# One product of 512 columns for the upper weights, in three stages of a two-block model

## The chip, the cores and the metric

The kernel runs on one core of one Trainium2 chip. The metric is the device time of one execution in microseconds (us), taken as the median of repeated runs; lower is better. The profile comes from one further execution.

## What is computed

The model has two blocks on 256 tokens of 1024 features (16 extra "meta" tokens are put in front of the first block, so that it works on 272). Everything is float32. Cut to what matters here:

```python
# first block, both layers: mixing, then an MLP; the MLP of layer 1 is touched by the change
a = relu(rmsnorm(h) @ w_up)              # 1024 -> 4096
h = h + (a * a) @ w_down                 # 4096 -> 1024

# second block, layer 0: short convolution
gb, gc, u = split(rmsnorm(x) @ w_in, 3)  # 1024 -> 3 x 1024
mix = (gb * causal_dwconv(gc * u, w_conv)) @ w_out

# second block, both layers: convolutional FFN
gate, up = split(causal_dwconv(rmsnorm(x) @ w_up, w_conv), 2)   # 1024 -> 2 x 2816
x = x + rmsnorm((silu(gate) * up) @ w_down)
```

## The kernel before

Every float32 matrix product is made of products in a reduced format (float32r). A number is split into an upper part and the rest: `hi` is the value copied into the format (ScalarE, L337 for weights, L362 for others) and `lo` is the value minus `hi` (VectorE, L338 and L363). A product is then hi·hi + hi·lo + lo·hi, all three added up in one PSUM bank by TensorE.

Two kinds of stages alternate. In the stages "weights stand still", a weight tile of 128 x 1024 holds eight blocks of 128 x 128; for each block `k` the helper `mm3` (L351) issues three products: upper weights by upper features (L352), upper weights by lower features (L353), lower weights by upper features (L354). The features lie with the feature number on the partitions, 256 tokens (272 in block one's first layer) in the columns, in the tiles `uh` and `ul`, so one weight tile costs 24 products of 256 columns and gives one tile of 128 outputs x 256 tokens in a PSUM bank. In the stages "features stand still" (`act_gemm`, L1123; helper `mm3a`, L357 to L359) 512 weight columns move past 128 tokens, so each product has 512 columns.

The weights come as a stream (`Stream`): 512 KB per weight tile by DMA into one of four `raw` buffers, split by ScalarE (L337) and VectorE (L338) some six tiles ahead, into eight pairs of buffers.

Stages that the change touches:

- `up1`: the MLP of layer 1, 32 weight tiles, `up_gemm(1, m, NM)` with `t0 = NM = 16`, PSUM name `pup`. The first four tiles are computed together, block by block, in the order in which `hg_split` (L426 on ScalarE for `uh`, L427 on VectorE for `ul`) finishes the features (L1098 to L1102). `relu_sq` (L923) drains each bank: relu (L925) and square (L926) on ScalarE, then the split into `ah` (L362, ScalarE) and `al` (L363, VectorE). The same helper serves layer 0 with 272 columns.
- `short_conv`: 16 of its 24 output tiles are weight-stationary (`psc`, helper `ws_tile`); the other 8 come from a features-stationary start (`first_tiles`, `pfb`).
- `conv_ffn`, twice: 18 gate tiles (`pg`) and 18 up tiles (`pu`) each; the first four of either kind come from `first_tiles`. A gate tile is drained by `conv`: a scaled copy (ScalarE L1284) and two shifted multiply-adds that read PSUM (VectorE L1285, L1286), then silu (ScalarE L1335). An up tile is drained by the same three, then GpSimd multiplies both (L1341), ScalarE splits off the upper part (`fah`, `fbh`, L362) and GpSimd the rest (L363).

All weight-stationary tiles of a stage take turns in four PSUM banks (tag `mm`). A bank is free for the tile after the next three when its last reader is done. The tile framework sets the waits and also fixes, before the run, the order of the instructions on each engine; instructions of several tiles are interleaved there, and each engine then takes its list in order and stops at an instruction whose input isn't ready.

The functions that the change touches:

Of the kernel before, what the change touches and what calls it, by code (L numbers as in the profile page):

```python
# [10 lines left out]
F32 = mybir.dt.float32  # L11
F32R = mybir.dt.float32r
I32 = mybir.dt.int32
AF = mybir.ActivationFunctionType
ALU = mybir.AluOpType
# [3 lines left out]
P = 128  # L19
D = 1024  # L20
KB = D // P
NM = 16
L = 272
# [250 lines left out]
def tile_forward(ctx: ExitStack, tc: tile.TileContext, wts, hT_in, pT_in, cols_in, rows_in, gsub_in, lam_in,  # L274
                 relb_in, consts_in, hot_in, out, dbg=None, stop=None):
    nc = tc.nc
    V, S, G, T = nc.vector, nc.scalar, nc.gpsimd, nc.tensor
# [11 lines left out]
    def ps(name="mm", tag="mm"):  # L289
        return banks["pool"].tile([P, 512], F32, tag=tag, name=name, bufs=banks["n"][tag])  # L290
# [58 lines left out]
    ws = Stream()  # L349

    def mm3(o, wh, wl, xh, xl, start, stop):  # L351
        T.matmul(o, wh, xh, start=start, stop=False)  # L352
        T.matmul(o, wh, xl, start=False, stop=False)  # L353
        T.matmul(o, wl, xh, start=False, stop=stop)  # L354

    def mm3a(o, xh, xl, wh, wl, start, stop):
        T.matmul(o, xh, wh, start=start, stop=False)  # L357
        T.matmul(o, xh, wl, start=False, stop=False)  # L358
        T.matmul(o, xl, wh, start=False, stop=stop)  # L359

    def split(hi, lo, src, eng=V):
        ins = S.activation(hi, src, AF.Copy)  # L362
        eng.tensor_tensor(lo, src, hi.bitcast(F32), ALU.subtract)  # L363
        return ins
# [4 lines left out]
    blk1 = ExitStack()  # L369
    main1 = blk1.enter_context(tc.tile_pool(name="main1", bufs=1, reuse_waits="tile"))  # L370
    h = main1.tile([P, KB, L], F32, name="h")
    uh = main1.tile([P, KB, L], F32R, name="uh")
    ul = main1.tile([P, KB, L], F32R, name="ul")
    R2 = main1.tile([P, L], F32, name="R2")
    mixs = ExitStack()
    ps1 = ExitStack()
# [491 lines left out]
    for pair in range(2):  # L868
        outs = [ps("pout", "mm" if m < 2 else "sm") for m in range(4)]
        for half in (1, 0):  # L870
            for j in range(2):
                wh, wl = ws.get("out", 2 * pair + j, half)
                for m in range(2):
                    o = outs[2 * j + m]
# [32 lines left out]
    def gain(name, i=0):  # L907
        g = xp.tile([P, D], F32, tag="gain", name="gain", bufs=2)
        nc.sync.dma_start(g, rows_in[row_of(name, i)].partition_broadcast(P))
        return g  # L910
# [11 lines left out]

    def relu_sq(o, m, t0):  # L923
        t = tmp1.tile([P, L], F32, tag="rl", name="rl", bufs=3)
        S.activation(t[:, t0:], o[:, t0:L], AF.Relu)  # L925
        S.activation(t[:, t0:], t[:, t0:], AF.Square)  # L926
        split(ah[m // 8][:, m % 8, t0:], al[m // 8][:, m % 8, t0:], t[:, t0:])

    def up_gemm(i, m, t0):
        wh, wl = ws.get(f"up{i}", m)  # L930
        o = ps("pup")
        for k in range(KB):
            mm3(o[:, t0:L], wh[:, k * P:(k + 1) * P], wl[:, k * P:(k + 1) * P], uh[:, k, t0:], ul[:, k, t0:], k == 0, k == KB - 1)
        relu_sq(o, m, t0)

    def split_p(raw, parts):
# [52 lines left out]
    for m in range(KB):  # L989
        o = ps("pdn")  # L990
        for g in range(4):
            wh, wl = ws.get("dn0", m, g)
# [3 lines left out]
        t = tmp1.tile([P, L], F32, tag="rl", name="dn", bufs=3)  # L996
# [44 lines left out]
    for g in (2, 3, 0, 1):  # L1041
        wh, wl = wp[g // 2]
        z = zs[g] = tmp2.tile([P, 2, L], F32, name=f"zp{g}")
        outs = []
        for m in range(2):
            o = ps("pz")
# [52 lines left out]
    for ks in ((0, 1), (2, 3), (6, 7, 4, 5)):  # L1099
        for (wh, wl), o in first:  # L1100
            for k in ks:
                mm3(o[:, NM:L], wh[:, k * P:(k + 1) * P], wl[:, k * P:(k + 1) * P], uh[:, k, NM:], ul[:, k, NM:], k == 0, k == 5)  # L1102
    for m in range(FF // P):
        if m < 4:
            relu_sq(first[m][1], m, NM)
# [79 lines left out]
    up_ = ctx.enter_context(tc.tile_pool(name="u2", bufs=1, reuse_waits="tile"))  # L1185
# [16 lines left out]
        return r  # L1202

    def new_u(name):
        return (up_.tile([P, KB, 256], F32R, tag="uh", name=name + "h", bufs=1),
                up_.tile([P, KB, 256], F32R, tag="ul", name=name + "l", bufs=1))

    def norm_T(u, t, g, r=None):

# [26 lines left out]
    def boundary(fin, u, g):  # L1236

        rr = []
        for t in range(2):
            with tc.high_priority(offset=HP):  # L1240
                fin(t)
                ins = norm_T(u, t, g)
            if t == 0:
                ws.cap = len(plan)
                with tc.issue_after(ins.ins):
                    ws.emit(ws.used + 6)
            rr.append(row_rstd(x[t]))
        return rr

    def half(a, t):  # L1250
        return a[:, :, t * P:(t + 1) * P]

    def ws_tile(key, u, o):

        wh, wl = ws.get(*key)
        for k in range(KB):
            mm3(o, wh[:, k * P:(k + 1) * P], wl[:, k * P:(k + 1) * P], u[0][:, k, :], u[1][:, k, :], k == 0, k == KB - 1)
        return o

    def first_tiles(key, ux, rr, u, g):  # L1260


        def mid():
            for t in range(2):
                norm_T(u, t, g, rr[t])

        acc = act_gemm(key, KB, lambda k, t: half(ux[0], t)[:, k], lambda k, t: half(ux[1], t)[:, k], KB, mid, bound=False)
        tok = []
        for t in range(2):
            y = big("ft")  # L1270
            for i, n in enumerate(H2):
                S.activation(y[:, n], acc[t][i], AF.Copy, scale=rr[t])
            tok.append(y)

        def block(n):
            o = ps("pfb", "acc")[:, 0:256]
            for t in range(2):
                T.transpose(o[:, t * P:(t + 1) * P], tok[t][:, n * P:(n + 1) * P], eye)
            return o
        return block  # L1280
# [7 lines left out]
    def short_conv(fin):  # L1288
        g = gain("g_pre_mix_2", 0)
        hs = ExitStack()  # L1290
        hp = hs.enter_context(tc.tile_pool(name="hidc", bufs=1, reuse_waits="tile"))
        sh = hp.tile([P, KB, 256], F32R, name="sh")
        sl = hp.tile([P, KB, 256], F32R, name="sl")
        rr = boundary(fin, (sh, sl), g)
        gp = gain("g_post_mix_2", 0)

        def tail(j, pc, pu, pb):
            gc = t2.tile([P, 256], F32, tag="f1", name="gc", bufs=3)
            S.activation(gc, pc, AF.Copy)
            V.tensor_tensor(gc, pu, gc, ALU.mult)  # L1300
            y = t2.tile([P, 256], F32, tag="f2", name="y", bufs=3)
            conv(y, gc, "sc", j)
            V.tensor_tensor(y, pb, y, ALU.mult)
            split(sh[:, j, :], sl[:, j, :], y)

        u = new_u("sc")
        block = first_tiles(("sc8",), (sh, sl), rr, u, g)
        for j in SC_ORDER:
            outs = []
            for part in (1, 2, 0):  # L1310
                if (j, part) in SC_FIRST:
                    outs.append(block(SC_FIRST.index((j, part))))
                else:
                    outs.append(ws_tile(("sci", j, part), u, ps("psc")[:, 0:256]))
            tail(j, *outs)
        acc = act_gemm(("sco",), KB, lambda k, t: half(sh, t)[:, k], lambda k, t: half(sl, t)[:, k], KB)
        hs.close()
        return post_fin(acc, gp)

    def conv_ffn(i, fin):  # L1320
        g = gain("g_pre_ffn_2", i)
        hs = ExitStack()
        hp = hs.enter_context(tc.tile_pool(name="hidf", bufs=1, reuse_waits="tile"))
        fa = [hp.tile([P, NF2 - KB, 256], F32R, name="fa" + c) for c in "hl"]
        ux = [hp.tile([P, KB, 256], F32R, name="fb" + c) for c in "hl"]

        def fpart(c, f):
            return fa[c][:, f, :] if f < NF2 - KB else ux[c][:, f - (NF2 - KB), :]
        rr = boundary(fin, ux, g)
        gp = gain("g_post_ffn_2", i)  # L1330

        def gate_tail(f, pg):
            a = t2.tile([P, 256], F32, tag="f1", name="a", bufs=3)
            conv(a, pg, f"fc{i}_", f)
            S.activation(a, a, AF.Silu)  # L1335
            return a

        def up_tail(f, pu, a):
            c = t2.tile([P, 256], F32, tag="f2", name="c", bufs=3)
            conv(c, pu, f"fc{i}_", NF2 + f)  # L1340
            G.tensor_tensor(c, c, a, ALU.mult)  # L1341
            split(fpart(0, f), fpart(1, f), c, G)

        u = new_u("ff")
        block = first_tiles(("ffu", i), ux, rr, u, g)
        for f in FFN_ORDER:
            a = gate_tail(f, block(f) if f < 4 else ws_tile(("gate", i, f), u, ps("pg")[:, 0:256]))
            up_tail(f, block(4 + f) if f < 4 else ws_tile(("upp", i, f), u, ps("pu")[:, 0:256]), a)
        acc = act_gemm(("ffd", i), NF2, lambda k, t: fpart(0, k)[:, t * P:(t + 1) * P],
                       lambda k, t: fpart(1, k)[:, t * P:(t + 1) * P], 6)  # L1350
        hs.close()
        return post_fin(acc, gp)
# [189 lines left out]
```

## Time and profile before

| | |
|---|---|
| median of 3 runs | 1258.46 us (1257.72 to 1258.51) |
| the profiled execution, its own time | 1255.57 us |
| span of its instructions | 1253.8 us |
| mean granted TensorE clock | 0.999 of full speed |
| TensorE busy | 1221.4 us of the span |
| VectorE, ScalarE, GpSimd busy | 824.1, 732.0, 216.9 us |

PE is TensorE, PEld its weight loads, DVE VectorE, ACT ScalarE, POOL GpSimd, SP the queue that issues most DMAs. A matmul's own duration overlaps that of the next one, so what a product costs in a stream is the step from one start to the next.

### The profile page before, as it was taken

Reading aid. Unit: us, or ns where it says so; the run is one execution under the profiler, and the core shown is the slowest. Engines: PE = TensorE matmul, PEld = TensorE weight load, DVE = VectorE, ACT = ScalarE, POOL = GpSimd, SP = SyncE. Lnnn points to the kernel's source line nnn. Section 1 sums busy time; section 2 is a strip of 40 time slices with the busy share of each in tenths; the row PEclk is TensorE's granted clock in tenths of the full one; section 3 lists DMA queues with packets and bytes.
Section 4 is the critical chain, followed back from the end, with each engine's and each line's share of the span. In section 5 each row is a group of like instructions: output and inputs, shape, how many; then the busy total and the mean of one; then the engine's idle time right before and its main releaser. Section 6 shows DMA issues by size and latency. Waiting matters only on the chain.

```text
span 1253.8 us, 21438 instructions
## 1 busy us (share of the span) xinstructions
PE 1221.4 (97%) x8250; PEld 1113.0 (89%) x8250; DVE 824.1 (66%) x1252; ACT 732.0 (58%) x1262; POOL 216.9 (17%) x184
## 2 busy tenths in 40 slices
PE   7999999999999999999999999999999999999997
PEld 7888899999997999887898899988789868999875
DVE  6775558555557755445775897754888867977455
ACT  7664458775345877433653676543677756765444
POOL 1454141000113000000000053410110010634001
PEclk9999999999999999999999999999999999999999
DMA  7432137555457755553753655554675337555542
GB/s 268 136 101 85 35 102 253 172 173 177 170 177 250 239 190 185 172 191 128 237 183 124 222 193 185 187 190 148 239 266 192 111 112 227 181 185 185 190 139 92
DMA packets 63461, 219.15 MB, mean 175 GB/s; under 512 B 7117, under 2 KB 9301, under 8 KB 63360
## 3 DMA queue, kind: packets, MB, share of 16 engines
q1 hardware_dynamic: 60192, 212.87, 50.5%
q10 hardware_dynamic: 2816, 4.20, 1.0%
q8 instruction: 65, 1.06, 0.3%
q0 software_dynamic: 352, 0.72, 0.2%
q14 instruction: 36, 0.29, 0.1%
HBM read 212.51 MB, written 5.26 MB: 174 GB/s over the span
## 4 chain that ended last, share of the span: by engine, by line
PE 83%; DVE 8%; issue 3%; ACT 2%; DMA 2%; POOL 2%; SPq 0%; DVEq 0%; POOLq 0%; ACTq 0%
PE acc L359 8%; PE acc L357 8%; PE acc L358 8%; PE pup L354 5%; PE pup L353 5%; PE pup L352 5%; PE pg L352 3%; PE pu L354 3%; PE pg L354 3%; PE pg L353 3%; PE pu L352 3%; PE pu L353 3%; PE pdn L352 3%; PE pdn L353 3%; PE pdn L354 3%
## 5 line engine op out<-in xcount | busy, mean ns | idle before, releaser
L338 DVE TENSOR_TENSOR lo<-raw,hi 128x1024 fp32r<-128x1024 f32 (+1 forms) x366 | 452.9, 1242 | 234.6 <-ACT hi L337 233.3
L337 ACT ACTIVATE hi<-raw 128x1024 fp32r<-128x1024 f32 (+1 forms) x380 | 398.3, 1055 | 251.5 <-PE acc L359 102.7
L352 PE MATMUL pup<-uh,hi 128*128 128x272 f32 (+1 forms) x512 | 146.1, 286 | 1.7 <-ACT uh L426 1.7
L354 PE MATMUL pup<-uh,lo 128*128 128x272 f32 (+1 forms) x512 | 146.1, 285 | 0.2 <-DVE lo L338 0.2
L353 PE MATMUL pup<-ul,hi 128*128 128x272 f32 (+1 forms) x512 | 145.8, 285 | 0.2 <-DVE ul L427 0.2
L1201 POOL TENSOR_TENSOR rs<-ss,mhalf 128x1 f32<-128x1 f32 x24 | 23.0, 960 | 485.1 <-DVE ss L1199 485.1
L352 PEld LDWEIGHTS pup<-uh,hi 128*128 128x128 f32 x512 | 96.4, 189 | 2.9 <-ACT uh L426 2.2
L354 PEld LDWEIGHTS pup<-uh,lo 128*128 128x128 f32 x512 | 96.6, 189 | 0.4 <-DVE lo L338 0.4
L353 PEld LDWEIGHTS pup<-ul,hi 128*128 128x128 f32 x512 | 96.3, 188 | 0.4 <-DVE ul L427 0.4
L1341 POOL TENSOR_TENSOR c<-c,a 128x256 f32<-128x256 f32 x44 | 59.7, 1357 | 132.7 <-DVE c L1286 132.7
L352 PE MATMUL pg<-ffh,hi 128*128 128x256 f32 x288 | 82.0, 285 | 0.0
L354 PE MATMUL pg<-ffh,lo 128*128 128x256 f32 x288 | 81.3, 282 | 0.0
L354 PE MATMUL pu<-ffh,lo 128*128 128x256 f32 x288 | 81.3, 282 | 0.0
L353 PE MATMUL pg<-ffl,hi 128*128 128x256 f32 x288 | 81.2, 282 | 0.0
L352 PE MATMUL pu<-ffh,hi 128*128 128x256 f32 x288 | 81.2, 282 | 0.0
L353 PE MATMUL pu<-ffl,hi 128*128 128x256 f32 x288 | 81.1, 282 | 0.0
L352 PE MATMUL pdn<-ah,hi 128*128 128x272 f32 x256 | 74.1, 290 | 0.0
L354 PE MATMUL pdn<-ah,lo 128*128 128x272 f32 x256 | 74.1, 289 | 0.0
L353 PE MATMUL pdn<-al,hi 128*128 128x272 f32 x256 | 73.7, 288 | 0.0
L353 PEld LDWEIGHTS pg<-ffl,hi 128*128 128x128 f32 x288 | 54.7, 190 | 0.1
L352 PEld LDWEIGHTS pg<-ffh,hi 128*128 128x128 f32 x288 | 54.7, 190 | 0.1
L354 PEld LDWEIGHTS pg<-ffh,lo 128*128 128x128 f32 x288 | 54.7, 190 | 0.0
(481 smaller groups left out, 3277.9 us busy)
## 6 DMA issues: line engine op xcount, KB each, us to landing
raw<-wts SPq DMA_DIRECT2D x378, 512.0 KB, 3.4
gain<-rows_in SPq DMA_DIRECT2D x13, 512.0 KB, 4.7
prj<-pe ACTq DMA_DIRECT2D x8, 256.0 KB, 6.2
pj<-prj SPq DMA_DIRECT2D x4, 512.0 KB, 5.0
out_dram<-x SPq DMA_DIRECT2D x8, 256.0 KB, 2.4
hank<-biasD ACTq DMA_DIRECT2D x4, 256.0 KB, 3.9
biasT<-bsb ACTq DMA_DIRECT2D x4, 256.0 KB, 3.5
biasb<-biasT SPq DMA_DIRECT2D x8, 128.0 KB, 2.7
```

The lines of the kernel that those rows point to most:

```text
L337: S.activation(hi[:, c], src[:, c], AF.Copy)
L338: (G if n in ON_POOL else V).tensor_tensor(lo[:, c], src[:, c], hi[:, c].bitcast(F32), ALU.subtract)
L352: T.matmul(o, wh, xh, start=start, stop=False)
L353: T.matmul(o, wh, xl, start=False, stop=False)
L354: T.matmul(o, wl, xh, start=False, stop=stop)
L357: T.matmul(o, xh, wh, start=start, stop=False)
L358: T.matmul(o, xh, wl, start=False, stop=False)
L359: T.matmul(o, xl, wh, start=False, stop=stop)
L1201: G.tensor_tensor(r, s[:, 3:4], mhalf[:, 0:1], ALU.pow)
L1341: G.tensor_tensor(c, c, a, ALU.mult)
```

## The change

A new helper `mm2` makes the two products with the upper weights into one of 512 columns: `uh` and `ul` become the two halves of one tile `u2`, and block `k` of both (two pieces of 256 columns) moves past the weights in one instruction, which writes both halves of the PSUM bank. The third product (lower weights by upper features) is added to the first half. A second helper, `add_halves`, then copies the second half to SBUF on ScalarE and adds the first half on VectorE. Both are used in the layer-1 `up1` stage, for the 16 `psc` tiles and for the gate tiles of both FFNs; the up tiles, the keys and queries and the layer-0 MLP keep `mm3`. In `relu_sq` the square moves from ScalarE to GpSimd where `mm2` is used. In `conv` of a gate tile the source becomes an SBUF tile.

```diff
+    def mm2(o, wh, wl, x2, start, stop):
+        T.matmul(o.rearrange("p (a t) -> p a t", a=2), wh, x2, start=start, stop=False)
+        T.matmul(o[:, 0:256], wl, x2[:, 0], start=False, stop=stop)
+
+    def add_halves(dst, o):
+        S.activation(dst, o[:, 256:512], AF.Copy)
+        V.tensor_tensor(dst, o[:, 0:256], dst, ALU.add)
...
-    uh = main1.tile([P, KB, L], F32R, name="uh")
-    ul = main1.tile([P, KB, L], F32R, name="ul")
+    u2 = main1.tile([P, 2, KB, L], F32R, name="u2")
+    uh, ul = u2[:, 0], u2[:, 1]
...
     def relu_sq(o, m, t0):
         t = tmp1.tile([P, L], F32, tag="rl", name="rl", bufs=3)
-        S.activation(t[:, t0:], o[:, t0:L], AF.Relu)
-        S.activation(t[:, t0:], t[:, t0:], AF.Square)
+        if t0:
+            add_halves(t[:, t0:], o)
+            S.activation(t[:, t0:], t[:, t0:], AF.Relu)
+            G.tensor_tensor(t[:, t0:], t[:, t0:], t[:, t0:], ALU.mult)
+        else:
+            S.activation(t, o[:, :L], AF.Relu)
+            S.activation(t, t, AF.Square)
         split(ah[m // 8][:, m % 8, t0:], al[m // 8][:, m % 8, t0:], t[:, t0:])
...
+            if t0:
+                mm2(o, *wk, u2[:, :, k, t0:], k == 0, k == KB - 1)
+            else:
+                mm3(o[:, :L], *wk, uh[:, k, :], ul[:, k, :], k == 0, k == KB - 1)
...
-                mm3(o[:, NM:L], wh[:, k * P:(k + 1) * P], wl[:, k * P:(k + 1) * P], uh[:, k, NM:], ul[:, k, NM:], k == 0, k == 5)
+                mm2(o, wh[:, k * P:(k + 1) * P], wl[:, k * P:(k + 1) * P], u2[:, :, k, NM:], k == 0, k == 5)
...
     def new_u(name):
-        return (up_.tile([P, KB, 256], F32R, tag="uh", name=name + "h", bufs=1),
-                up_.tile([P, KB, 256], F32R, tag="ul", name=name + "l", bufs=1))
+        u = up_.tile([P, 2, KB, 256], F32R, tag="u", name=name, bufs=1)
+        return u[:, 0], u[:, 1], u
...
+    def ws_pair(key, u, name, pool):
+        wh, wl = ws.get(*key)
+        o = ps(name)
+        for k in range(KB):
+            mm2(o, wh[:, k * P:(k + 1) * P], wl[:, k * P:(k + 1) * P], u[2][:, :, k, :], k == 0, k == KB - 1)
+        s = pool.tile([P, 256], F32, tag="f0", name="s" + name, bufs=4)
+        add_halves(s, o)
+        return s
...
-                    outs.append(ws_tile(("sci", j, part), u, ps("psc")[:, 0:256]))
+                    outs.append(ws_pair(("sci", j, part), u, "psc", hp))
...
-            a = gate_tail(f, block(f) if f < 4 else ws_tile(("gate", i, f), u, ps("pg")[:, 0:256]))
+            a = gate_tail(f, block(f) if f < 4 else ws_pair(("gate", i, f), u, "pg", hp))
```

## Rows read from the trace of the kernel before

**Rows 1.** The page, part 1: busy time of the engines.
```profile
PE 1221.4 (97%) x8250; PEld 1113.0 (89%) x8250; DVE 824.1 (66%) x1252; ACT 732.0 (58%) x1262; POOL 216.9 (17%) x184
```
**Rows 2.** The page, part 4: the chain that ended last, by engine.
```profile
PE 83%; DVE 8%; issue 3%; ACT 2%; DMA 2%; POOL 2%; SPq 0%; DVEq 0%; POOLq 0%; ACTq 0%
```
**Rows 3.** Windows: stretch, length, busy time (instructions) by engine, clock, DMA.
```profile
430.00:490.00 60.00, 60.00 (x510) 60.00 (x509) 33.92 (x43) 45.89 (x86) 0.00 (x0) 1.00 0.58 192
520.00:580.00 60.00, 60.00 (x262) 48.97 (x261) 25.44 (x21) 21.22 (x20) 0.00 (x0) 1.00 0.56 189
755.00:815.00 60.00, 60.00 (x506) 60.00 (x505) 43.02 (x63) 35.74 (x63) 24.79 (x22) 1.00 0.55 185
640.00:664.00 24.00, 24.00 (x204) 24.00 (x203) 16.67 (x25) 11.91 (x19) 0.00 (x0) 1.00 0.52 176
```
**Rows 4.** Groups by form, whole span: the products with the upper weights.
```profile
L353 PE MATMUL pg<-ffl,hi 128*128 128x256 f32 x288 | 81.2, 282 | 0.0
L353 PE MATMUL pup<-ul,hi 128*128 128x256 f32 x256 | 72.1, 282 | 0.2 <-DVE ul L427 0.2
L353 PE MATMUL psc<-scl,hi 128*128 128x256 f32 x128 | 36.1, 282 | 0.0
```
**Rows 5.** Timeline of TensorE, 519.8 to 521 us: start, duration, instruction.
```profile
519.79 0.39 PE L357 MATMUL acc<-hi,ah 128*128 128x512 f32 x1
...
520.92 0.39 PE L359 MATMUL acc<-hi,al 128*128 128x512 f32 x1
```
**Rows 6.** Groups by form, 424 to 495 us (`up1`): DVE and ACT.
```profile
L338 DVE TENSOR_TENSOR lo<-raw,hi 128x1024 fp32r<-128x1024 f32 x26 | 31.9, 1226 | 28.7 <-ACT hi L337 28.5
L337 ACT ACTIVATE hi<-raw 128x1024 fp32r<-128x1024 f32 x26 | 27.6, 1060 | 14.5 <-PE pup L353 14.5
L363 DVE TENSOR_TENSOR al<-rl,ah 128x256 fp32r<-128x256 f32 x26 | 11.0, 424 | 0.0
L926 ACT ACTIVATE rl<-rl 128x256 f32<-128x256 f32 x25 | 10.5, 419 | 0.8
L925 ACT ACTIVATE rl<-pup 128x256 f32<-128x256 f32 x26 | 9.5, 366 | 0.0
```
**Rows 7.** Groups, 752 to 815 us (first FFN): waits of ACT and DVE.
```profile
L1285 DVE SCALAR_TENSOR_TENSOR a<-pg,cols,a 128x255 f32<-128x255 f32 x11 | 5.3, 483 | 16.6 <-ACT a L1284 16.6
...
L362 ACT ACTIVATE fbh<-c 128x256 fp32r<-128x256 f32 x6 | 2.5, 418 | 11.9 <-POOL c L1341 11.9
```
**Rows 8.** Timelines of ACT, DVE, POOL and PE, 762 to 770 us (first FFN).
```profile
763.32 0.42 ACT L362 ACTIVATE fah<-c 128x256 fp32r<-128x256 f32 x1 [1.98 <-POOL c L1341]
...
764.20 0.48 DVE L1285 SCALAR_TENSOR_TENSOR a<-pg,cols,a 128x255 f32<-128x255 f32 x1 [1.51 <-ACT a L1284]
765.12 1.22 DVE L338 TENSOR_TENSOR lo<-raw,hi 128x1024 fp32r<-128x1024 f32 x1
765.26 0.28 PE L354 MATMUL pg<-ffh,lo 128*128 128x256 f32 x1
765.30 0.42 ACT L1335 ACTIVATE a<-a 128x256 f32<-128x256 f32 x1 [0.25 <-DVE a L1286]
766.25 0.48 DVE L1285 SCALAR_TENSOR_TENSOR c<-pu,cols,c 128x255 f32<-128x255 f32 x1
767.39 1.58 POOL L1341 TENSOR_TENSOR c<-c,a 128x256 f32<-128x256 f32 x1 [2.84 <-DVE c L1286]
769.00 0.42 ACT L362 ACTIVATE fah<-c 128x256 fp32r<-128x256 f32 x1 [1.98 <-POOL c L1341]
769.33 0.46 ACT L1284 ACTIVATE a<-pg,cols 128x256 f32<-128x256 f32 x1
```
**Rows 9.** Timeline of POOL, 732 us: a product with no split beside it.
```profile
732.81 0.73 POOL L1341 TENSOR_TENSOR c<-c,a 128x256 f32<-128x256 f32 x1 [0.92 <-DVE c L1286]
```
**Rows 10.** Timelines of ACT and DVE, 407 to 412 us (start of `up1`).
```profile
407.63 3.31 ACT L426 ACTIVATE uh<-h,cols 128x256 fp32r<-128x256 f32 x8 [0.55 <-DVE h L1087]
...
408.33 3.24 DVE L427 SCALAR_TENSOR_TENSOR ul<-h,cols,uh 128x256 fp32r<-128x256 f32 x8
```

More of the change, by code (lines that the diff above doesn't have):

```diff
@@ L932, in up_gemm @@
         for k in range(KB):
-            mm3(o[:, t0:L], wh[:, k * P:(k + 1) * P], wl[:, k * P:(k + 1) * P], uh[:, k, t0:], ul[:, k, t0:], k == 0, k == KB - 1)
+            wk = wh[:, k * P:(k + 1) * P], wl[:, k * P:(k + 1) * P]
+            if t0:
+                mm2(o, *wk, u2[:, :, k, t0:], k == 0, k == KB - 1)
+            else:
+                mm3(o[:, :L], *wk, uh[:, k, :], ul[:, k, :], k == 0, k == KB - 1)
         relu_sq(o, m, t0)
```

## Prediction

> **What bounds the kernel now.** I read the page from the top. TensorE is busy 1221.4 of 1253.8 us, the other engines far less [rows 1], and the chain that ended last runs through TensorE for 83% of the span [rows 2]; the reader should see that time can only be won where a TensorE instruction becomes cheaper, and lost where TensorE is made to wait. A busy share doesn't say what a product costs, since durations overlap, so I counted products in stretches of pure work [rows 3]. A stretch also counts the one or two products that are under way at its start, so I take two off. The layer-1 up products: 60 us / 508 = 118.1 ns from start to start. The FFN's products of 256 columns: 60 / 504 = 119.0. The short convolution's: 24 / 202 = 118.8. Products of 512 columns: 60 / 260 = 230.8. TensorE is busy through all four stretches and the granted clock is 1.00, its 2.4 GHz level; nothing is waited for there.
>
> The last views are those of the engines that drain the banks. In `up1` ScalarE works 45.9 of 60 us and VectorE 33.9; in the short convolution 11.9 and 16.7 of 24; in the FFN 35.7 and 43.0 of 60, with GpSimd 24.8 [rows 3]. So there is room in sum, but the FFN is a stage in which ScalarE and VectorE wait for each other, below.
>
> **The change on TensorE.** Each block that `mm2` takes loses one product: 256 in `up1`, 288 gate, 128 short convolution, one for each L353 instruction [rows 4], 672 in all. Two products of 256 columns become one of 512. What is saved is twice the short step minus the long one: in `up1` 236.2 − 230.8 = 5.4 ns, in the short convolution 6.8, in the FFN 7.2. That gives 256 × 5.4 + 128 × 6.8 + 288 × 7.2 = 1.4 + 0.9 + 2.1 = **4.4 us saved**. The trace of before has no product of 512 columns whose moving operand lies in two pieces, as `u2[:, :, k]` does. Bounds: nothing, if the second piece costs as much as a new product; and 672 × (5.4 to 7.2 + 4.8) = 7.6 us, if the long product runs at the fastest spacing seen, five steps in 1.13 us, 226 ns [rows 5]. I take 4.4, since the long stretch is an average over work like this.
>
> [...]
>
> **The start of `up1`.** The features come from ScalarE at one `uh` per 0.41 us from 407.63, and from VectorE at one `ul` per 0.41 us from 408.33 [rows 10]. Before, the first products needed only the first `uh`; now the first needs the first `ul` too, done at about 408.75 instead of 408.05. After that TensorE has four tiles' work per block and is behind the features. I take **0.5 us lost**; above, if the wait covers the last write into the joint tile (411.57), 3.5 us. In the other stages the features are complete long before, as features-stationary products stand between.
>
> **What the draining costs.** There are 32 + 36 + 16 = 84 new pairs of a copy and an add. The copy reads 256 columns from PSUM like L925, 0.37 us; the add is like L363's, 0.42 us [rows 6].
>
> In `up1` ScalarE's list per tile is now weights' upper part 1.06, relu 0.37, square 0.42, split about 0.42: 2.27 us [rows 6]. Copy in, square out leaves 2.22. VectorE goes from 1.23 + 0.42 to 2.07. GpSimd, idle there [rows 3], gets a square of 0.73 to 1.58 us, by GpSimd's product without and with a weight split of VectorE beside it [rows 8, 9]. A tile lasts 24 × 118.1 ns = 2.83 us, later 2.79. All fit under it. What covers them is the four banks: a bank is asked for again three tiles, 8.4 us, after its product ended, while the chain to its last reader is 0.8 us plus what it queues behind (a split of 1.06 and one of 1.23). I take nothing. In the short convolution three copies and three adds come to 24.0 / 202 × 72 = 8.5 us of TensorE work; VectorE goes from 5.9 to 7.2 us there. Nothing, again; at its end the longer tail (0.8 us) hides behind the seven earlier blocks of the next product, 7 × 6 × 0.23 = 9.7 us.
>
> **The FFN is the doubtful stage.** Follow one round [rows 8]: split 763.32, then the gate's convolution on ScalarE 0.33 later, VectorE's two steps from 764.20, a weight split at 765.12, the up tile's steps from 766.25, GpSimd at 767.39, and ScalarE's next split at 769.00, which it had waited 1.98 us for. This is a ring with no slack in it, 5.68 us long, and TensorE's round is 48 × 119.0 = 5.71 us. So the drain already runs as slowly as TensorE, 3.8 us behind it (the gate's product at 765.26 ends at 765.54; its convolution starts at 769.33). After the change TensorE's round is 5.65 us. Where the copy and the add go in the ring decides. In every round ScalarE waits 1.98 us for GpSimd and VectorE 1.5 us for the convolution [rows 7, 8], in the same stretch, and the gate's product is long done. If the copy stands ahead of that split, both fit into these waits and the ring keeps 5.68; 14 rounds at 0.03 us over TensorE's are taken up by the banks. I take this, cost nothing.
>
> **Sum.** 1255.57 − 4.4 + 0.5 = 1251.7 for the profiled execution. The median of the runs stands 2.9 us above that execution, so **1254.6 us**, 0.3% less. About 0.2%, 2.5 us, is what a measurement of this kernel tells from no change.
>
> **Rivals.**
>
> *The copy stands behind the split in ScalarE's list* (slower). Then copy, add and two hand-overs (0.1 each, as convolution to VectorE's step) lengthen the ring by 0.37 + 0.42 + 0.2 = 1.0 us at most; by less if the weight split at 765.12 moves into the new wait. From 5.65 us on the ring sets TensorE's pace. The banks give slack first: the up tile's last reader ends about 4.5 us after its product, and the bank is asked for after 8.5, so 4.0 us. With two thirds of the 1.0: (6.35 − 5.65) × 14 − 4.0 = 5.8 us per FFN, 11.6 for both: 1266. The whole 1.0 gives 1276, a half 1261. For it: today's list holds exactly such a split that waits ahead of the next gate's convolution. Against it: the copy depends on TensorE alone. Chance 0.24.
>
> *The long product costs as much as the two short ones*, its step being set by columns only or the two pieces costing a start each. Then 1258.5 + 0.5 = 1259.0, no change. For it: the short step scatters by 0.9 ns between the stages [rows 3], doubled 1.8 of the 5 to 7 ns that are to be saved. Against it: the 512-column stretch is below twice the short step in all three stages. [...] Chance 0.2.
>
> *`up1` loses its cover*: ScalarE's list in the strict order copy, relu, split of one tile, with the waits for VectorE and GpSimd in it. Then a tile costs ScalarE 1.06 + 0.37 + 0.42 + 0.42 + 0.73 + 0.42 and four hand-overs, 3.8 us, against 2.79: 32 × 1.0 − 8.4 = 24 us more, 1279. Against it: lists of several tiles are interleaved already [rows 8]. Chance 0.04.
>
> **Chances and range.** The forecast has 0.52; its own range is 1251 to 1257, of which a little lies within 0.2% of before. So faster 0.48, same 0.25, slower 0.27. The range goes from 1258.46 − 7.6 = 1250.9 up to 1268: it leaves out the top of the first rival, the third, and something better than the fastest spacing.
>
> **What would show it.** In the profile of the changed kernel: products of 512 columns into `pup`, `pg`, `psc` with steps of about 231 ns followed by one of 119; a block at 350 ns instead of 356. In the FFN the time from one `fah` split to the next, and whether the copy from `pg` stands before or after the split; TensorE idle in `pg` or `pu` products with a release by ScalarE or VectorE would be the first rival, idle in `pup` the third. The prediction is wrong if the long step is over 236 ns, if the FFN's round is above 5.7 us, or if the first products of `up1` start after 409.3.

## The result

The changed kernel takes 1298.41 us (median of 4 runs, 1297.9 to 1304.15) against 1258.09 for the kernel before, measured beside it: 40 us slower, ratio 1.0337, 95% interval 1.0309 to 1.0365 (ratios here go by all runs, not by the medians). The forecast was 1254.6, with a range up to 1268. Its sign was wrong, and the range doesn't hold the time.

The page of the changed kernel, its first part (busy time) and its fourth (the chain that ended last, by engine):

```profile
PE 1228.2 (95%) x7578; PEld 1081.8 (83%) x7578; DVE 857.3 (66%) x1336; ACT 746.4 (58%) x1314; POOL 246.3 (19%) x216
...
PE 64%; DVE 14%; ACT 8%; issue 6%; POOL 5%; DMA 2%; DVEq 0%; SPq 0%; POOLq 0%; ACTq 0%
```

The 672 products are gone (8250 to 7578 [rows 1]), yet the chain runs through TensorE for 64% of a longer span, 83% before [rows 2]; VectorE, ScalarE and GpSimd took most of the difference. The windows of the changed kernel, on stretches like those of [rows 3]:

```profile
430.00:490.00 60.00, 57.38 (x320) 48.53 (x319) 40.56 (x57) 37.20 (x76) 17.03 (x19) 1.00 0.54 171
533.00:593.00 60.00, 60.00 (x262) 48.99 (x261) 25.74 (x21) 21.75 (x21) 0.00 (x0) 1.00 0.61 193
654.00:678.00 24.00, 24.00 (x138) 20.93 (x138) 20.34 (x36) 14.57 (x27) 0.00 (x0) 1.00 0.55 177
768.00:828.00 60.00, 52.22 (x357) 47.71 (x358) 39.21 (x64) 33.80 (x62) 19.87 (x18) 1.00 0.49 157
```

In `up1` and in the FFN TensorE now has holes, 2.6 and 7.8 us in 60. No engine is full in their place: the busiest, VectorE, works 40.6 and 39.2 of 60 us, and ScalarE does *less* per 60 us than before in both stages. The short convolution is as dense as ever, and so is the features-stationary stretch. The clock is at its upper level in all four.

Where the 42 us between the two profiled spans lie, stage by stage. I took each stage from the start of its first product to the end of its last one in TensorE's timeline, and the stretches between; the first line is the length before, the others the difference to it, in us, from one profiled execution of each kernel. The lines below the second are the experiments.

| kernel | up1 | up1 to short conv. | short conv. | FFN 0 | FFN 0 to keys | FFN 1 |
|---|---|---|---|---|---|---|
| before (length) | 91.5 | 117.0 | 48.0 | 104.8 | 114.1 | 104.9 |
| **after** | +4.2 | +8.7 | −1.0 | +12.9 | +3.0 | +13.3 |
| gemm_only | −1.8 | +0.1 | −0.9 | +0.3 | +3.0 | −1.1 |
| drain_only | +4.2 | +8.1 | 0.0 | +11.8 | 0.0 | +12.4 |
| joint_tiles | +0.1 | +0.1 | 0.0 | 0.0 | +1.5 | 0.0 |
| psc_only | 0.0 | 0.0 | −1.0 | 0.0 | +3.0 | 0.0 |
| copy_first | +4.1 | +8.9 | −1.0 | +1.1 | +1.6 | +1.1 |
| late_split | +4.4 | +7.5 | −1.0 | +0.9 | +3.1 | +0.7 |
| square_act | −1.8 | 0.0 | −1.0 | +12.7 | +1.5 | +13.4 |
| vec_halves | −1.8 | −0.1 | −0.9 | +4.7 | +1.6 | +4.6 |
| square_pool | +0.2 | +10.6 | 0.0 | 0.0 | 0.0 | 0.0 |
| up1_and_sc | −0.4 | 0.0 | −1.0 | 0.0 | 0.0 | 0.0 |
| all_three | −0.2 | 0.0 | −1.0 | +1.2 | 0.0 | +1.0 |

In the changed kernel the short convolution gains 1.0, and three places lose: `up1` with its aftermath 12.9, the FFNs 26.2, the boundary to keys and values 3.0. The stretch ahead of `up1` differs by 11 us between these executions: its first product starts between 406.9 us (joint_tiles) and 417.9 us (late_split). In the two latest, drain_only and late_split, the granted clock was lower for a part of the stretch (0.55 and 0.54 in the ten microseconds from 130, 1.00 there in the kernel before). So the table starts at `up1`, and differences of one or two us are read from it rather than from the medians.

**The FFN round.** Timelines of ScalarE, VectorE, GpSimd and TensorE in the changed kernel, one round, which answers to [rows 8] (start, duration, instruction; in brackets how long the engine had been idle, and what ended that):

```profile
780.59 0.42 ACT L371 ACTIVATE fah<-c 128x256 fp32r<-128x256 f32 x1 [1.64 <-POOL c L1369]
780.91 1.04 ACT L337 ACTIVATE hi<-raw 128x1024 fp32r<-128x1024 f32 x1
781.86 0.37 ACT L362 ACTIVATE spg<-pg 128x256 f32<-128x256 f32 x1
783.58 0.51 ACT L1312 ACTIVATE a<-spg,cols 128x256 f32<-128x256 f32 x1 [1.36 <-DVE spg L363]
...
787.61 0.42 ACT L371 ACTIVATE fah<-c 128x256 fp32r<-128x256 f32 x1 [1.64 <-POOL c L1369]
...
781.99 1.23 DVE L338 TENSOR_TENSOR lo<-raw,hi 128x1024 fp32r<-128x1024 f32 x1 [2.03 <-ACT hi L337]
783.13 0.42 DVE L363 TENSOR_TENSOR spg<-pg,spg 128x256 f32<-128x256 f32 x1
...
785.77 1.22 DVE L338 TENSOR_TENSOR lo<-raw,hi 128x1024 fp32r<-128x1024 f32 x1
...
786.05 1.53 POOL L1369 TENSOR_TENSOR c<-c,a 128x256 f32<-128x256 f32 x1 [4.22 <-ACT a L1363]
...
783.60 0.51 PE L358 MATMUL pg<-ff,hi 128*128 128x512 f32 x1 [0.88 <-DVE spg L363]
```

From split to split it is 7.02 us (787.61 − 780.59), and the eight rounds behind it are 7.02 or 7.03 long; before, 5.68. Read ScalarE's list: split, weights' upper part, *then* the copy, then a wait of 1.36 us for the add, which stands on VectorE behind the lower part of those weights. Only then the convolution, silu, GpSimd's product, and the next split. The convolution began 0.33 us after the split before; it begins 2.99 us after it now. TensorE waits 0.88 us for the add (the last line), which is the bank's last reader.

**The round of `up1`.** Timelines of ScalarE, VectorE and GpSimd in the changed kernel:

```profile
459.18 0.36 ACT L362 ACTIVATE rl<-pup 128x256 f32<-128x256 f32 x1
460.89 0.42 ACT L936 ACTIVATE rl<-rl 128x256 f32<-128x256 f32 x1 [1.36 <-DVE rl L363]
...
464.29 0.42 ACT L371 ACTIVATE ah<-rl 128x256 fp32r<-128x256 f32 x1 [1.15 <-POOL rl L937]
464.62 1.04 ACT L337 ACTIVATE hi<-raw 128x1024 fp32r<-128x1024 f32 x1
465.57 0.36 ACT L362 ACTIVATE rl<-pup 128x256 f32<-128x256 f32 x1
...
459.30 1.23 DVE L338 TENSOR_TENSOR lo<-raw,hi 128x1024 fp32r<-128x1024 f32 x1 [0.53 <-ACT hi L337]
...
463.22 1.04 POOL L937 TENSOR_TENSOR rl<-rl 128x256 f32<-128x256 f32 x1 [1.21 <-ACT rl L936]
```

Two tiles take 465.57 − 459.18 = 6.39 us, 3.2 each, against TensorE's 2.8. ScalarE waits twice: 1.36 us for the add behind a weight split, 1.15 us for GpSimd's square. TensorE ran ahead on its four banks at first, so only 4.2 us show inside the stage; the other 8.7 come after it. TensorE's weight loads there, and windows of the changed kernel:

```profile
508.04 0.31 PEld L1172 LDWEIGHTS pth<-eye,h 128*128 128x128 f32 x3 [2.83 <-ACT ah L371]
511.16 0.50 PEld L1137 LDWEIGHTS pst<-ones,ssum 128*128 128x128 f32 x2 [2.81 <-DVE r2t L1138]
...
510.00:520.00 10.00, 8.84 (x34) 7.58 (x35) 4.19 (x13) 6.20 (x12) 1.23 (x2) 0.66 0.29 105
```

Two things make up the 8.7. The next stage's first steps wait 2.83 and 2.81 us for ScalarE and VectorE, which are still busy with the last tiles. Then TensorE goes on at a granted clock of 0.66, two thirds of these ten microseconds at its lower level (1.2 GHz); in the kernel before it is 1.00 there. By my estimate, half of the time that it works at the lower level, that costs between 2 and 3 us. So some 10 of the 12.9 us are the ring itself: from the first tile's split to the last tile's it takes 93.2 us instead of 83.1.

### The profile page after: what moved, and what is told of

The parts are those of the page before. It is cut to its first block, busy times and chain, and to the rows that moved or that the text cites. A ratio compares the mean times of both kernels' runs of the same rounds, so it can differ in the third digit from the quotient of the medians.

```text
span 1296.1 us, 20191 instructions
## 1 busy us (share of the span) xinstructions
PE 1228.2 (95%) x7578; PEld 1081.8 (83%) x7578; DVE 857.3 (66%) x1336; ACT 746.4 (58%) x1314; POOL 246.3 (19%) x216
## 4 chain that ended last, share of the span: by engine, by line
PE 64%; DVE 14%; ACT 8%; issue 6%; POOL 5%; DMA 2%; DVEq 0%; SPq 0%; POOLq 0%; ACTq 0%
PE acc L368 8%; PE acc L366 8%; PE acc L367 8%; DVE lo L338 5%; ACT hi L337 4%; POOL c L1369 3%; PE pdn L352 2%; PE pdn L353 2%; PE pdn L354 2%; PE pup L352 2%; PE pup L354 2%; PE pup L353 2%; PE psc L358 2%; POOL rl L937 1%; PE ptf L1236 1%
## 5 line engine op out<-in xcount | busy, mean ns | idle before, releaser
L358 PE MATMUL pg<-ff,hi 128*128 128x512 f32 x288 | 105.0, 403 | 19.3 <-DVE spg L363 19.3
L358 PE MATMUL pup<-u,hi 128*128 128x512 f32 x256 | 91.3, 398 | 5.4 <-DVE rl L363 2.4
L352 PE MATMUL pu<-ff,hi 128*128 128x256 f32 x288 | 81.3, 282 | 3.5 <-ACT a L1363 3.5
L353 PE MATMUL pu<-ff,hi 128*128 128x256 f32 x288 | 81.2, 282 | 0.0
L354 PE MATMUL pu<-ff,lo 128*128 128x256 f32 x288 | 81.2, 282 | 0.0
L359 PE MATMUL pg<-ff,lo 128*128 128x256 f32 x288 | 80.8, 281 | 0.0
L352 PE MATMUL pup<-u,hi 128*128 128x272 f32 x256 | 74.6, 291 | 0.0
L354 PE MATMUL pup<-u,lo 128*128 128x272 f32 x256 | 74.2, 290 | 0.3 <-DVE lo L338 0.3
L353 PE MATMUL pup<-u,hi 128*128 128x272 f32 x256 | 73.7, 288 | 0.0
L359 PE MATMUL pup<-u,lo 128*128 128x256 f32 x256 | 71.8, 280 | 0.0
L352 PEld LDWEIGHTS pu<-ff,hi 128*128 128x128 f32 x288 | 54.3, 189 | 6.1 <-ACT a L1363 4.7
L353 PEld LDWEIGHTS pu<-ff,hi 128*128 128x128 f32 x288 | 54.4, 189 | 0.0
L354 PEld LDWEIGHTS pu<-ff,lo 128*128 128x128 f32 x288 | 54.3, 189 | 0.0
```

The costliest lines, as they stand in the source:

```text
L358: T.matmul(o.rearrange("p (a t) -> p a t", a=2), wh, x2, start=start, stop=False)
L359: T.matmul(o[:, 0:256], wl, x2[:, 0], start=False, stop=stop)
```

## The experiments

**gemm_only.** The products of the change without its drain.

```diff
-            add_halves(t[:, t0:], o)
-            S.activation(t[:, t0:], t[:, t0:], AF.Relu)
-            G.tensor_tensor(t[:, t0:], t[:, t0:], t[:, t0:], ALU.mult)
+            S.activation(t[:, t0:], o[:, 0:256], AF.Relu)
+            S.activation(t[:, t0:], t[:, t0:], AF.Square)
...
-        s = pool.tile([P, 256], F32, tag="f0", name="s" + name, bufs=4)
-        add_halves(s, o)
-        return s
+        return o[:, 0:256]
```

> Leaves out the hi·lo part of the sum: the products are those of the change (one of 512 columns, one of 256), but each bank is drained as in the kernel before, from its first half alone, without the copy, the add and the square on GpSimd. Theory A (the new drain makes the loss, and the 512-column products do save): up1 and both FFN stages run at TensorE's pace again, FFN round 5.63 to 5.68 us, and the time is 1258.1 - 4.4 + 0.5 = 1254, plus up to 3 us that the joint tile costs at the keys-and-values boundary: 1254 to 1257. Theory B (the 512-column products or the joint feature tile make the loss): it stays above 1285.

Measured: 1257.86 us, ratio 0.9988 (0.9965 to 1.0012), 0.9 us above the range of theory A and far from B. Windows in the two FFNs:

```profile
755.00:815.00 60.00, 59.51 (x417) 55.44 (x416) 43.80 (x64) 36.26 (x64) 23.27 (x20) 1.00 0.60 185
1100.00:1150.00 50.00, 50.00 (x356) 46.90 (x354) 35.75 (x54) 29.96 (x52) 20.92 (x18) 1.00 0.60 192
```

The splits are 5.68 to 5.70 us apart in the steady part of both stages, as before (but for two of 5.9 and 6.0 us in FFN 0), although TensorE needs only 5.65 for a round now. In FFN 1 it works through the window without a hole, runs ahead of the drain on its banks and keeps the whole saving (−1.1); in FFN 0 it has holes (0.49 us in this window), its rounds are as long as the drain's, and nothing is gained. Three up tiles of FFN 0 take 3.0 to 3.4 us instead of 2.85, 1.0 us in sum; what lengthens them isn't shown. The boundary to keys loses 3.0 us in this kernel too, without any new drain.

**drain_only.** The drain of the change without its products.

```diff
+    def add_halves(dst, o):
+        S.activation(dst, o, AF.Copy)
+        V.tensor_tensor(dst, o, dst, ALU.max)
...
+            add_halves(t[:, t0:], o[:, t0:L])
+            S.activation(t[:, t0:], t[:, t0:], AF.Relu)
+            G.tensor_tensor(t[:, t0:], t[:, t0:], t[:, t0:], ALU.mult)
```

> The products and the separate feature tiles of the kernel before; only the new drain: a copy of the bank to SBUF on ScalarE, then on VectorE the larger of bank and copy (which are equal), then the rest as in the change, with the square on GpSimd. Theory A (the drain makes the loss): FFN round about 7.0 us, up1 about 3.2 us per tile, and a time of about 1258 + 13 + 13 + 13 = 1297 (1294 to 1299), without the 3 us at the keys-and-values boundary and without the saving. Theory B (products or joint tile): 1258 to 1262.

Measured: 1294.17 us, ratio 1.0289 (1.0253 to 1.0325). Theory A: +12.3 in and behind `up1`, +11.8 and +12.4 in the FFNs, a split every 7.03 us, nothing at the boundary to keys. Nearly the whole loss without one 512-column product. (The 12.3 again hold a stretch at the lower clock: 0.82 in the ten microseconds from 520.)

**joint_tiles** and **psc_only.** The joint feature tile alone, and the change in the short convolution alone.

```diff
-        return (up_.tile([P, KB, 256], F32R, tag="uh", name=name + "h", bufs=1),
-                up_.tile([P, KB, 256], F32R, tag="ul", name=name + "l", bufs=1))
+        u = up_.tile([P, 2, KB, 256], F32R, tag="u", name=name, bufs=1)
+        return u[:, 0], u[:, 1], u
```

> The kernel before with its features in one joint tile of two halves, in up1 and in the second block, and nothing else changed. Theory A: the tile is taken as one buffer, so that whatever starts early with one half now waits for both: 3 us later at the boundary to keys and values, 1261, nothing elsewhere. Rival: the 3 us come from the drains' order there, and this kernel is 1258, no change.

> The change in the short convolution alone (16 output tiles, with copy and add), with the joint tiles; up1 and the FFNs as in the kernel before. Theory A: this stage had room, its products go from 48.0 to 47.1 us, so -0.9 us there, plus what the joint tile costs at the keys-and-values boundary: 1257.2 without that cost, 1260 with it. Rival (any such drain slows its stage): above 1262.

Measured: 1260.06 us, ratio 1.0008 (0.9982 to 1.0033), and 1260.36, ratio 1.0014 (0.9994 to 1.0034): neither can be told from no change by its time. By the table the joint tile loses 1.5 us at the boundary, and 3.0 with the short convolution's change in the same program. TensorE's first product on the keys' features in joint_tiles, ScalarE ahead of it, and TensorE's next wait:

```profile
907.68 0.50 PE L357 MATMUL acc<-hi,kv 128*128 128x512 f32 x1 [1.27 <-ACT kv L362]
...
905.83 1.31 ACT L1371 ACTIVATE sgm<-acc,rs 128x512 f32<-128x512 f32 x2 [1.70 <-PE acc L359]
907.04 0.59 ACT L362 ACTIVATE kv<-ptf 128x512 fp32r<-128x512 f32 x1
...
909.78 0.73 PE L359 MATMUL acc<-hi,kv 128*128 128x512 f32 x2 [0.90 <-DVE kv L363]
```

Both sigmoids stand ahead of the first split there; before, that split stood between them. TensorE waits 1.27 us for it instead of 0.62, and 0.90 us for the lower part where it didn't wait before: together the 1.5 us. So an order on ScalarE moved because two tiles became one. Kernels that keep two tiles at this boundary (drain_only, square_pool, up1_and_sc, all_three) lose nothing. The kernels that lose 3.0 have the same two waits; what differs is the clock behind them. Windows of joint_tiles and of psc_only:

```profile
907.00:917.00 10.00, 8.42 (x39) 6.65 (x40) 9.91 (x18) 8.45 (x17) 0.64 (x2) 1.00 0.79 256
...
907.00:917.00 10.00, 8.34 (x32) 6.54 (x33) 8.65 (x16) 8.56 (x17) 0.70 (x2) 0.83 0.80 260
```

The granted clock is 0.83 behind the waits in the four kernels that lose 3.0 or 3.1 (the changed one, gemm_only, psc_only, late_split) and 1.00 in the four that lose 1.5 or 1.6 (joint_tiles, copy_first, square_act, vec_halves). Why it falls in one kernel and holds in another isn't settled.

**copy_first** and **late_split.** The change, with the FFN's split of a gated product pinned behind another instruction of ScalarE: behind the next tile's copy, or behind the next pair's first convolution steps.

```diff
+            pg = block(f) if f < 4 else ws_pair(("gate", i, f), u, "pg", hp)
+            if late:
+                with tc.issue_after(copies[-1].ins):
+                    split(*late, G)
+            a = gate_tail(f, pg)
```

> The change with one thing altered, in the FFNs: the split of a gated product is put behind the copy of the next gate tile in ScalarE's list, so that the order is weights' split, copy, split, convolution in place of split, weights' split, copy, wait for the add, convolution. Theory A (copy and add inside the ring split, copy, add, convolution, silu, GpSimd's product, split lengthen it to 7.02 us): the round falls to TensorE's 5.65 or the 5.7 of before, both FFNs win 13 us each, 1298 - 26 = 1272, and up1 stays as it is. Rival B (VectorE and GpSimd have too much work with the added operations, whatever the order): the round stays above 6.5 and the time above 1288.

> The change with one thing altered, in the FFNs: the split of a gated product is put behind the convolution's first steps of the next gate and up tile in ScalarE's list, so that no convolution waits for GpSimd any more and the ring is opened. Theory A: TensorE sets the pace, 5.63 to 5.66 us a round, 1270 to 1272, not slower than with the copy alone put first. Rival B (load of VectorE and GpSimd): round above 6.5, above 1288.

Measured: 1274.96 us, ratio 1.0134 (1.0108 to 1.0159), and 1277.13, ratio 1.0148 (1.0111 to 1.0184). Theory A in both for the stage, though the times lie 3 and 5 us above what was expected. The FFNs lose 1.1 and 1.1, or 0.9 and 0.7, in place of 13. In late_split the splits are 5.85 us apart, neither the 5.63 to 5.66 of theory A nor the 6.5 of its rival; what sets that pace isn't shown. Its four times go from 1271 to 1281 at granted clocks of 0.994 to 0.985, so the table tells more than its median. Timelines of ScalarE and GpSimd in copy_first:

```profile
817.77 0.42 ACT L373 ACTIVATE fbh<-c 128x256 fp32r<-128x256 f32 x1 [0.43 <-POOL c L1371]
819.18 0.51 ACT L1314 ACTIVATE a<-spg,cols 128x256 f32<-128x256 f32 x1 [1.00 <-DVE spg L365]
...
821.48 1.05 ACT L337 ACTIVATE hi<-raw 128x1024 fp32r<-128x1024 f32 x1
822.44 0.36 ACT L364 ACTIVATE spg<-pg 128x256 f32<-128x256 f32 x1
823.22 0.42 ACT L373 ACTIVATE fbh<-c 128x256 fp32r<-128x256 f32 x1 [0.42 <-POOL c L1371]
...
821.65 1.53 POOL L1371 TENSOR_TENSOR c<-c,a 128x256 f32<-128x256 f32 x1 [2.25 <-ACT a L1365]
```

The copy and the weights' upper part now lie in the time in which GpSimd multiplies; the round is 5.45 us, shorter than TensorE's, while the drain catches up. What is left of the loss comes while the first eight tiles are drained: two gate tiles last 3.6 and 4.1 us instead of 2.8, 2 us in sum.

**square_act** and **square_pool.** The square of `up1` moved alone: back to ScalarE in the changed kernel, over to GpSimd in the kernel before.

```diff
-            G.tensor_tensor(t[:, t0:], t[:, t0:], t[:, t0:], ALU.mult)
+            S.activation(t[:, t0:], t[:, t0:], AF.Square)
```

> The change with the square of up1 back on ScalarE, nothing else altered. Theory A (the crossing to GpSimd and back sets up1's 3.2 us per tile): ScalarE's own steps come to 2.2 to 2.4 us, a tile is back at 2.8, up1 wins up to 13 us, 1285. Rival B (the crossing to VectorE for the add, behind a weight split of 1.23, sets it, or ScalarE's list with the square is as long): up1 stays above 3.0 us per tile, 1292 or more.

> The kernel before with the square of up1 on GpSimd and nothing else altered (no copy, no add, no 512-column product). Theory A1 (the crossing to GpSimd and back is by itself what makes up1 slow: in a strict list weights' split 0.95, relu 0.32, GpSimd 0.62 to 1.35, split 0.33 and two hand-overs make 2.4 to 3.2 us a tile): above 3.0 us per tile, 1266 to 1271. Theory A2 (it takes the copy and the add in the same list too): 2.84 us per tile, 1258.

Measured: square_act 1283.99 us, ratio 1.0231 (1.0185 to 1.0277); square_pool 1267.42, ratio 1.0086 (1.0054 to 1.0117). Theories A and A1: the square alone is enough for most of `up1`'s loss. With it on ScalarE the stage is 1.8 us *shorter* than before, copy and add and all; with it on GpSimd the old drain's stage and aftermath are 10.8 us longer, a stretch at the lower clock included (0.68 and 0.81 in the twenty microseconds from 500). Timelines of ScalarE, VectorE and GpSimd in square_pool:

```profile
461.22 0.42 ACT L362 ACTIVATE ah<-rl 128x256 fp32r<-128x256 f32 x1 [1.49 <-POOL rl L927]
461.54 1.04 ACT L337 ACTIVATE hi<-raw 128x1024 fp32r<-128x1024 f32 x1
462.49 0.36 ACT L925 ACTIVATE rl<-pup 128x256 f32<-128x256 f32 x1
464.35 0.42 ACT L362 ACTIVATE ah<-rl 128x256 fp32r<-128x256 f32 x1 [1.49 <-POOL rl L927]
...
462.62 1.23 DVE L338 TENSOR_TENSOR lo<-raw,hi 128x1024 fp32r<-128x1024 f32 x1 [0.52 <-ACT hi L337]
...
462.93 1.38 POOL L927 TENSOR_TENSOR rl<-rl 128x256 f32<-128x256 f32 x1 [1.75 <-ACT rl L925]
```

The ring is 464.35 − 461.22 = 3.13 us: split, weights' upper part, relu, GpSimd, split. Nothing is interleaved between relu and split, since the list puts the wait there.

**vec_halves.** The change with the square on ScalarE and the copy on VectorE.

```diff
-        S.activation(dst, o[:, 256:512], AF.Copy)
+        V.tensor_copy(dst, o[:, 256:512])
```

> The change with the square on ScalarE and the copy of the second half on VectorE in place of ScalarE, so that copy and add follow each other on one engine. Theory A (hand-overs in a ring, not the added work, make the loss): up1 falls to 2.8 us per tile; in the FFN no copy stands behind the split any more, and the round falls to 5.7 to 6.0: 1259 to 1268. Rival B (VectorE's load): VectorE has 0.42 us more per tile than in the change, both stages stay slow, 1290 or more.

Measured: 1267.94 us, ratio 1.0083 (1.0053 to 1.0112), at the top of theory A's bounds. `up1` is right (−1.8), the FFN half right: its round is 6.29 us, more than I had said. Timelines of ScalarE and GpSimd:

```profile
771.46 0.42 ACT L371 ACTIVATE fah<-c 128x256 fp32r<-128x256 f32 x1 [1.98 <-POOL c L1369]
771.78 1.04 ACT L337 ACTIVATE hi<-raw 128x1024 fp32r<-128x1024 f32 x1
772.73 0.49 ACT L1312 ACTIVATE a<-spg,cols 128x256 f32<-128x256 f32 x1
...
775.85 1.87 POOL L1369 TENSOR_TENSOR c<-c,a 128x256 f32<-128x256 f32 x1 [3.17 <-ACT a L1363]
```

The copy no longer stands in the ring, but a weight split does (771.78, between split and convolution, where 0.33 us lay before), and GpSimd's product meets another on VectorE and takes 1.87 us. It is the position in the list that counts, for old instructions as for new ones.

**up1_and_sc** and **all_three.** What is left when the rings are mended: the change in `up1` (square on ScalarE) and the short convolution, without or with the FFNs (copy ahead of the split); joint tiles in each stage's own pool, two tiles at the boundary to keys.

```diff
-        u = new_u("sc")
+        u = pair_u("sc", hp)
```

> The change in up1 (with the square on ScalarE) and in the short convolution alone; the FFNs as before; the joint tile of the short convolution lies in that stage's own pool, so that the boundary to keys and values has its two separate tiles again. Theory A (what saves is up1's -1.8 and the short convolution's -0.9, the joint tile costs the 1.5 to 3.0 us at the keys-and-values boundary, and 0.5 us is lost at the start of up1): -2.2 us, 1256, with no loss at that boundary. Rival (the 3 us there come from something else): it is lost there again and the time is 1258 to 1260.

> All three stages with the 512-column product: up1 with the square on ScalarE, the short convolution, and the FFNs with the copy put ahead of the split; joint tiles in each stage's own pool. Theory A: -2.2 us as without the FFNs, plus 1.1 us per FFN, which is the saving of 1.0 less 2 us of TensorE waits while the first eight tiles are drained: 1258, no change from the kernel before. Rival (loads add up once all stages have the new drain): above 1265.

Measured: 1256.6 us, ratio 0.9995 (0.9972 to 1.0019), and 1258.6, ratio 1.0003 (0.9974 to 1.0032). The terms are as forecast but for `up1`, which gained only 0.4 and 0.2 in these profiles (the reason is in the last section). Neither kernel can be told from the one before: by the table the 512-column product is worth some 2 us of 1258 here, and the FFNs give theirs back.

## Why the prediction was wrong

- *TensorE saves 4.4 us*: the price per product was right, the sum wasn't. `gemm_only` shows 0.9 in the short convolution, 128 × 6.8 ns, the figure predicted; 1.8 in `up1` (1.4 predicted; the rest belongs to the next point); but 0.8 in both FFNs together instead of 2.1: all of it in FFN 1, nothing in FFN 0. The ring of 5.68 us [rows 8] stood just above TensorE's new round; I had both numbers side by side, and let the banks take up the difference, which they did in one FFN of the two. Most of what FFN 0 lacks lies in three long tiles, whose cause is open. A block takes 0.35 us, as the timeline of TensorE at the start of `up1` shows:

```profile
409.17 0.50 PE L358 MATMUL pup<-u,hi 128*128 128x512 f32 x1 [2.42 <-DVE u L436]
...
410.03 0.39 PE L358 MATMUL pup<-u,hi 128*128 128x512 f32 x1
410.26 0.28 PE L359 MATMUL pup<-u,lo 128*128 128x256 f32 x1
410.38 0.39 PE L358 MATMUL pup<-u,hi 128*128 128x512 f32 x1
```

  The second rival (a long product costs two short ones) falls by this.
- *The start of `up1`, 0.5 us lost*: right for the first product, at 409.17: 1.0 later than before, of which 0.5 is that the features began later (ScalarE at 408.09 instead of 407.63). But before, TensorE also waited for features behind its first products; the first four tiles now take 11.2 us instead of 11.8, of which the cheaper products make 0.2, so the stage gets back some 0.4 of this loss.
- *Draining `up1`, "I take nothing"*: the first step that failed. I added up each engine's list, found that all fit under 2.8 us, and let four banks cover the chain. But it is a ring, not a chain: the list puts a wait for GpSimd ahead of the next weight split, and so a tile costs ScalarE the wait as well. (3.2 − 2.8) × 32 = 12.8 us; measured 12.9, but that they agree is luck: the ring itself costs some 10, and the lower clock behind the wait, which no term of mine had, most of the rest. Banks don't pay for that; they move it to the end of the stage. The third rival was this mechanism; I priced it at 3.8 us a tile less 8.4 us of banks and gave it 0.04. square_pool shows that the square alone is enough for such a ring (3.13 us).
- *Draining the short convolution, nothing*: right (−1.0 with copy and add).
- *The FFN, "if the copy stands ahead of that split … I take this, cost nothing"*: the second step that failed, and the larger one. The copy stands behind the split: the first rival. Its size was off too. I had "1.0 us at most"; the ring grew by 1.34. The way from split to convolution grew by 2.66, because the weights' upper part (0.95 from start to start) stands between split and copy, and their lower part on VectorE between copy and add; the way from there to the next split shrank by 1.32, as a weight split that stood in it before moved into the new wait. With that, (7.02 − 5.65) × 14 − 4.0 = 15, less the 1 saved: 14; measured 13. That copy_first gives back 12 of it by one changed position shows the cause.
- *The boundary to keys and values*: not in the prediction at all. 3.0 us: 1.5 of waits from the joint tile, as joint_tiles shows, and about as much from a granted clock of 0.83 behind them.

## What to carry to other kernels

Where engines hand work round in a ring within a tile, price an added operation by where it will stand in each engine's list, and by what stands between it and its neighbours there, not by whether each engine has room in sum; a ring whose length equals TensorE's round has no room, whatever the busy shares say. Buffers between the stages delay such a loss to the end of the stage and don't remove it when the next stage needs everything. An operation moved off a busy engine onto an idle one can lose more than it weighs if the busy engine then waits for it in its list: here moving 0.42 us of work a tile cost 11 us in 32 tiles. And a wait of TensorE can cost more than its length, when the clock is lower behind it.

## What the hardware showed besides

**GpSimd and VectorE block each other.** GpSimd's product of 256 columns takes 0.73 us alone [rows 9] and, in the lines shown, 1.53 to 1.87 beside a weight split of VectorE. In the FFN round above the split runs from 785.77 to 786.99; the product begins at 786.05 and ends 0.59 us after the split's end. It goes the other way too, in copy_first's timelines of VectorE and GpSimd, where the product is first:

```profile
757.07 1.75 DVE L338 TENSOR_TENSOR lo<-raw,hi 128x1024 fp32r<-128x1024 f32 x1
758.75 0.95 DVE L1315 SCALAR_TENSOR_TENSOR a<-spg,cols,a 128x255 f32<-128x255 f32 x1
...
756.03 1.71 POOL L1371 TENSOR_TENSOR c<-c,a 128x256 f32<-128x256 f32 x1
758.27 1.15 POOL L374 TENSOR_TENSOR fal<-c,fah 128x256 fp32r<-128x256 f32 x1 [0.53 <-ACT fah L373]
```

The split takes 1.75 us instead of 1.22, and a convolution step 0.95 instead of 0.48. The Trainium skill says why ("SBUF — State Buffer", section "SBUF: two separate sides"): the two engines share a port pair, which the one that starts first holds for its whole instruction when the VectorE operation has two inputs in SBUF. In the two cases above the trace agrees. In the lines of vec_halves it is less clear: there the product is recorded at 775.85, VectorE's split only at 775.91, and the product is held up all the same. Either way an operation on an idle GpSimd costs more in a stage where VectorE splits weights than it does alone.

**The clock can fall behind a wait.** Behind `up1` it did so in each of the five kernels in which TensorE had to wait there for the slow drain (the changed one, drain_only, copy_first, late_split, square_pool), and in none of the other eight. At the start of `up1` it is less regular. In all_three, windows ahead of and at the start of `up1`:

```profile
400.00:410.00 10.00, 7.07 (x31) 5.40 (x30) 8.92 (x18) 6.50 (x13) 0.00 (x0) 1.00 0.99 357
410.00:420.00 10.00, 10.00 (x50) 8.68 (x49) 8.42 (x17) 8.16 (x17) 0.00 (x0) 0.83 0.60 217
```

After a stretch in which TensorE worked 7.07 of 10 us, its granted clock is 0.83 in the next 10 us, so a third of them at the lower level (1.2 GHz), 50 products in place of 59. At half a block, 0.175 us, a product that is 9 × 0.175 = 1.6 us, just what `up1` gains less in this kernel than in square_act, which has the same stage. up1_and_sc shows the same. The changed kernel's clock held at 1.00 there, with 7.58 us of work ahead of it, and square_act's with 7.25; what decides whether it falls wasn't settled. For a change worth two microseconds such a fall decides what one sees.
